# Two 256-column halves for every 512-column three-pass matmul in a hybrid decoder layer

## The chip, the cores and the metric

The kernel runs on one core of a Trainium2 chip. Its engines work side by side: TensorE multiplies matrices into PSUM, whose eight banks each hold 512 float32 columns on 128 partitions; VectorE and ScalarE read PSUM and SBUF and write the results back; GpSimd and SyncE issue most of the DMA transfers. The metric is the device time of one execution in microseconds, taken as the median of the runs.

## The reference, cut to what matters

One decoder layer for 512 tokens of width 2048, all in float32. Two attention branches (a sparse one that keeps 128 keys per query, and a dense one with a latent projection) are gated, summed and projected, and a convolutional feed-forward part of width 5632 follows:

```python
proj = h @ w_in                                   # 2048 x 7568
o_a = dsa_attention(qa, ka, va, qi, ki, wi * IDX_W_SCALE)
o_b = causal_dense_attention(mq, mk, mv)
merged = sigmoid(gate_a) * (o_a @ w_pa) + sigmoid(gate_b) * (o_b @ w_pb)
x = x + gt_a * (merged @ w_o)
u = h @ w_up                                      # 2048 x 11264
x = x + gt_f * ((silu(gate) * val) @ w_down)      # gate, val: causal convolution of u
```

Each `@` is a product that needs more precision than one fast pass of TensorE gives.

## The kernel before, in words

**Three passes.** The kernel's fast matmul format is `float32r`, a float32 of reduced precision. Every operand of the large products is split into a high part (a ScalarE copy that rounds to `float32r`) and a low part (a VectorE subtraction, the rest): `wtile` does it for weights at lines 110 and 111, `split` for activations at lines 117 and 118. `mm3` (lines 120 to 123) then adds three products into one PSUM region: high by high (line 121), high by low (line 122), low by high (line 123). Its arguments are the PSUM region `o`, the stationary pair `lh, ll` (at most 128 columns), the moving pair `rh, rl` (as many columns as `o`), and two flags: `first` starts a new sum, `last` ends it. Each matmul is one weight load of the stationary operand and one stream of the moving operand.

**Who calls it.** `lin_fm` makes blocks of 128 output features by all 512 tokens: the weights are stationary and the activations move, 512 columns. It does the branch gates, the two branch projections and `w_up`. `lin_tm` makes blocks of 128 tokens by up to 512 output features: the activations are stationary and the weights move. It does `w_o`, `w_down`, the query projection and the latents with 512 columns, and two narrower ones, 320 columns of `w_in` and 384 of `w_mq_up`. Both walk over the contraction in steps of one weight tile of up to 1104 columns, and over four banks within each step. `quarter_k` does the first part of `w_in` in the order of a written plan, while the modulation columns are still being computed. The indexer calls `mm3` with 64 rows and 256, 384 or 512 columns.

**Staging.** A weight tile is loaded by SyncE into one of five raw buffers, then split into one of three pairs of high and low buffers. The four banks `bank[0:4]` and the four `bank[4:8]` alternate between output blocks; in the attention parts the second four serve attention. When a block's contraction is done, ScalarE or VectorE empties its bank (`conv` at line 1085 for `w_up`, line 1118 for `w_down`).

**Order.** The program is written in one order, and the framework plans the order on each engine from a modelled timeline when the kernel is built; weight tiles get a priority that lets them go far ahead. In the attention parts (about 230 to 1050 us) matmuls of `mm3`, transposes and plain float32 matmuls of attention (lines 669, 677, 693, 932 to 935) alternate on TensorE. From 1050 us on the stream is almost all `mm3`; lines 752 and 753 are two single-operand matmuls that serve the modulation columns, and line 1041 transposes before the second norm. These call TensorE directly and not through `mm3`.

Of the kernel before, what the change touches and what calls it, by code (L numbers as in the profile page):

```python
# [31 lines left out]
def trunk_layer_kernel(  # L32
# [22 lines left out]
    V, A, G, PE, SP = nc.vector, nc.scalar, nc.gpsimd, nc.tensor, nc.sync  # L55
# [3 lines left out]
    psum = ctx.enter_context(tc.tile_pool(name="psum", bufs=1, space=bass.MemoryType.PSUM))  # L59
    dram = ctx.enter_context(tc.tile_pool(name="scratch", bufs=1, space=bass.MemoryType.DRAM))  # L60

# [1 line left out]
    cur = [None] * n_slots  # L63
    free = deque(range(n_slots))
    held = {}
# [1 line left out]
    def get(dt=F32):  # L67
        i = free.popleft()
        if cur[i] is None or cur[i].dtype != dt:
            cur[i] = pool.tile([P, T], dt, name=f"slot{i}", tag=f"slot{i}")  # L70
        held[id(cur[i])] = i
        return cur[i]

    def getr():
        return get(F32R)
# [42 lines left out]
        V.tensor_tensor(dst_lo, src, r32(dst_hi), ALU.subtract)  # L118

    def mm3(o, lh, ll, rh, rl, first, last):  # L120
        PE.matmul(o, lh, rh, start=first, stop=False)  # L121
        PE.matmul(o, lh, rl, start=False, stop=False)  # L122
        PE.matmul(o, ll, rh, start=False, stop=last)  # L123

    def lin_fm(src, c0, act, K, banks, evac, tick=None, M=4):
        kn = 8 // M
        for kg in range(0, K, kn):
            wh, wl = wtile(src, kg, kn, c0, M * P)
            for m in range(M):
                ms = slice(m * P, (m + 1) * P)  # L130
                for i in range(kn):
                    k = kg + i
                    ah, al = act[k]
                    mm3(banks[m], wh[:, i, ms], wl[:, i, ms], ah, al, k == 0, k == K - 1)
                if kg + kn == K:
                    evac(m, banks[m])
            if tick:
                tick()

    def lin_tm(src, c0, n, act, K, banks, evac, k0=0, tick=None):  # L140
        for kg in range(0, K, 2):
            wh, wl = wtile(src, k0 + kg, 2, c0, n)
            for tb in range(4):
                ts = slice(tb * P, (tb + 1) * P)
                for i in range(2):
                    k = kg + i
                    ah, al = act[k]
                    mm3(banks[tb][:, :n], ah[:, ts], al[:, ts], wh[:, i, :], wl[:, i, :],
                        k == 0, k == K - 1)
                if kg + 2 == K:  # L150
                    evac(tb, banks[tb][:, :n])
            if tick:
                tick()
# [2 lines left out]
        cnt["half"] += 1  # L156
        return bank[4:8] if cnt["half"] % 2 == 0 else bank[0:4]

# [1 line left out]
    ident = pool.tile([P, P], F32, name="ident")  # L160
    make_identity(nc, ident)
    ones = pool.tile([P, 1], F32, name="ones")
# [45 lines left out]
    c_act = pool.tile([P, KD], F32, name="c_act")  # L208
    PE.transpose(bank[7][:, 0:16], v1[0:16, P:2 * P], ident[0:16, 0:16])
    A.activation(c_act, bank[7][:, 0:16], AF.Silu)  # L210
    # causal bias: zeros, then the triangle of the diagonal block
    zslot = get()
    Z = zslot[:, 0:256].bitcast(BF)
    G.memset(Z, 0.0)
# [5 lines left out]
        V.tensor_scalar(v, ss, 1.0 / n, EPS, op0=ALU.mult, op1=ALU.add)  # L220
        G.tensor_tensor(dst, v, mhalf[:, :w], ALU.pow)

# [1 line left out]
    ssx = pool.tile([P, 16], F32, name="ssx")  # L224
    rstd = pool.tile([P, 4], F32, name="rstd")
    junk = get()
# [37 lines left out]
    for r in xs:  # L264
        put(*r)

# [1 line left out]
    mod = pool.tile([P, 96], F32, name="mod")  # L268
    s_a = pool.tile([P, KD], F32, name="s_a")
    s_f = pool.tile([P, KD], F32, name="s_f")  # L270
# [39 lines left out]
        V.scalar_tensor_tensor(s_a[:, 2 * g:2 * g + 2], mod[:, 16 + 2 * g:18 + 2 * g], 1.0,  # L310
                               col1[:, 96 + 2 * g:98 + 2 * g], op0=ALU.add, op1=ALU.mult)

    # input projection in quarters of the contraction: A = indexer, B = sparse k/v and part of the gates
    part = {"A": [get() for _ in range(7)], "B": [get() for _ in range(7)]}

    def quarter_k(j, w):
# [19 lines left out]
        if name == "A":  # L336
            for tb in range(1, 4):
                ts = slice(tb * P, (tb + 1) * P)
                for cb in range(2):
                    ns = slice(cb * 512, (cb + 1) * 512)  # L340
                    i = (tb - 1) * 2 + cb
                    mm3(bank[i], hh[:, ts], hl[:, ts], wh[:, ns], wl[:, ns], first, last)
                    fin(i, bank[i])
            mm3(bank[6][0:80, :], wh[:, 1024:1104], wl[:, 1024:1104], hh, hl, first, last)
            fin(6, bank[6][0:80, :], 80)
        else:
            for tb in range(4):
                ts = slice(tb * P, (tb + 1) * P)
                mm3(bank[tb], hh[:, ts], hl[:, ts], wh[:, 0:512], wl[:, 0:512], first, last)
                fin(tb, bank[tb])  # L350
            for m in range(3):
                ms = slice(512 + m * P, 512 + (m + 1) * P)
                mm3(bank[4 + m], wh[:, ms], wl[:, ms], hh, hl, first, last)
                fin(4 + m, bank[4 + m])
# [59 lines left out]
    V.tensor_copy(wcv, bank[7][:, 0:352].rearrange("p (j n) -> p j n", j=4))  # L414
    put(v2)

# [1 line left out]
    pos_f = gslot[0:4, 384:384 + P]  # L418
    V.tensor_copy(pos_f, posi)
    PE.transpose(bank[7][:, 256:260], pos_f, ident[0:4, 0:4])  # L420
# [73 lines left out]
        cnt["at"] += 1  # L494
        return AT[cnt["at"] % 4]

# [1 line left out]
    kit = part["A"][6]  # L498
    kw_tm = tslot[3][:, 0:320].rearrange("p (t n) -> p t n", t=4)
    kdup = tslot[4].rearrange("p (t a d) -> p t a d", t=4, a=2)  # L500
# [20 lines left out]
    for tb in range(1, 4):  # L521
        S = (tb + 1) * P
        qiT = []
        for cb in range(2):
# [5 lines left out]
            o = (getr(), getr())  # L530
# [4 lines left out]
        rl = [get(), get(), get()]  # L535
# [38 lines left out]
    put(*kiT, tslot[3], tslot[4])  # L574
    mask[0] = Z[:, 384:512]

# [1 line left out]
    sq = [get(), get()]  # L578

    def head_ss(dst, src3, i):  # L580
# [47 lines left out]
    for cb in range(2):  # L628
        lin_tm(w_in, C_QA + cb * 512, 512, h, KD, MM, ev_qa(cb))

# [1 line left out]
    att = {}  # L632

    def attend_bufs():
# [67 lines left out]
    put(mslot, tslot[0])  # L702
    attend_free()

# [1 line left out]
    ada_blocks = [8, 9, 10, 11, 16, 17, 18, 19, 12, 13, 14, 15, 20, 21, 22, 23]  # L706
    gst = [get(), get()]
    ada_acc = [get(), get()]
# [1 line left out]
    def ada_stream():  # L710
        for n, cb in enumerate(ada_blocks):
            assert len(pend) < 2
            acc = ada_acc[n % 2]
            for kp in range(8):
                t = raw_tile()[:, 0:1024].rearrange("p (k n) -> p k n", k=2)
                SP.dma_start(t, w_ada[kp * 2 * P:(kp + 1) * 2 * P, cb * 512:(cb + 1) * 512]
                             .rearrange("(k p) n -> p k n", p=P))
                for i in range(2):
                    k = kp * 2 + i
                    if k == 0:  # L720
                        V.tensor_scalar(acc, t[:, i], c_act[:, 0:1], None, op0=ALU.mult)
                    else:
                        V.scalar_tensor_tensor(acc, t[:, i], c_act[:, k:k + 1], acc,  # L723
                                               op0=ALU.mult, op1=ALU.add)
                yield None
            pend.append((cb, acc))
            done[0] += 1
            if done[0] == 12:
                yield None
# [3 lines left out]
    stream = ada_stream()  # L733
# [33 lines left out]
    def reload(d):  # L767
        pairs = []
        for dh, dl in d:
            th, tl = getr(), getr()  # L770
            G.dma_start(th, dh)
            G.dma_start(tl, dl)
            pairs.append((th, tl))
        return pairs

# [1 line left out]
    gate_d = [dram.tile([P, T], F32, name=f"gate{k}") for k in range(2 * KD)]  # L777
    for m in range(3):
        G.dma_start(gate_d[m], part["B"][4 + m])
# [17 lines left out]
    for n in range(GA1):  # L797
        gate_block(n)

# [1 line left out]
    krot = pool.tile([P, 4, 64], F32, name="krot")  # L801
    ss_kr = pool.tile([P, 4], F32, name="ss_kr")
    kvT = [(getr(), getr()) for _ in range(2)]
# [38 lines left out]
    lat_T(ml2, mqT, gmq)  # L842
    put(*ml2)

# [1 line left out]
    pairs = {}  # L846

    def up_pair(hp):
# [92 lines left out]
        put(*qT)  # L941
        put(*kTr, *qTr)

    # first branch projection, kept in DRAM
    pa_d = [dram.tile([P, T], F32, name=f"pa{k}") for k in range(KD)]

    def pa_block(cb):
# [24 lines left out]
    put(*gst)  # L972
    put(tslot[1], tslot[2], zslot)

# [1 line left out]
    ob = reload(ob_d) + [tuple(att["o"][0:2]), tuple(att["o"][2:4])]  # L976
    mg = []

# [30 lines left out]
    for t in ob:  # L1009
        put(*t)  # L1010

# [1 line left out]
    ss1 = pool.tile([P, 16], F32, name="ss1x")  # L1013
    x1_d = [[dram.tile([P, T], F32, name=f"x1_{db}_{tb}") for tb in range(4)] for db in range(4)]
    x1 = []
# [62 lines left out]
        put(t)  # L1078
    put(rbc2)

# [1 line left out]

    def conv(j, b):
        t = get()
# [105 lines left out]
```

## Time and profile before

| what | value |
|---|---|
| median of 2 runs | 2796.87 us (2795.78 to 2797.96) |
| span of the profiled execution | 2791.8 us |
| TensorE matmuls | 12,160, busy 2753.4 us (99%) |
| TensorE weight loads | 12,160, busy 2204.5 us (79%) |
| VectorE, ScalarE, GpSimd | busy 56%, 32%, 6% |
| memory read and written | 376.93 MB and 30.41 MB, 146 GB/s |

The profile is one execution. A line of a group names the source line, the engine, the operation, output and inputs by the program's names, the shapes, the count, then busy time and mean duration of one, and the idle time before. Matmuls are pipelined: a matmul's record reaches from its start to its modelled end, and the next one starts earlier than that. So durations overlap, and the rate is read from the distances between starts. PEld is TensorE's weight load, which has its own rows. "Issue" is a wait for nothing that the profile shows.

The profiled execution's own time isn't listed apart from its span; the median lies 5.1 us above the span, for what comes ahead of the first and behind the last recorded instruction.

### The profile page before, as it was taken

The page shows a single profiled execution, that of the slowest core. Times are in us where ns is not written, and L with a number is a line of the kernel's source. Part 1 is how long each engine was busy: PE and PEld are TensorE (multiplying, and loading weights), DVE is VectorE, ACT ScalarE, POOL GpSimd, SP SyncE. Part 2 cuts the span into 40 slices and gives each one's busy share as a digit, 9 for nine tenths or more (in the row PEclk, how much of TensorE's full clock was granted, in tenths as well). Part 3 has the DMA queues.
Part 4 walks back from the last instruction along what each step waited for, and adds up shares of the span by engine and source line. Part 5 has one row for each costly group of instructions (what it writes and reads, how often), then busy time and mean ns, then how long its engine had stood idle before and what let it go on. Part 6 is the DMA issues. An engine that isn't in the chain of part 4 may idle for free.

```text
span 2791.8 us, 31818 instructions
## 1 busy us (share of the span) xinstructions
PE 2753.4 (99%) x12160; PEld 2204.5 (79%) x12160; DVE 1550.7 (56%) x2615; ACT 903.2 (32%) x1309; POOL 177.5 (6%) x355
## 2 busy tenths in 40 slices
PE   6999999999999999999999999999999999999999
PEld 5877777788887768887888888888888888888887
DVE  7987975544467658546444353635263544434357
ACT  4333433322344553224333222222223231313231
POOL 1000100100031231000000000000000000000010
PEclk8999999999999999999999999999999999999999
DMA  9942245655464587645333433334343333333352
GB/s 321 362 138 87 68 138 176 203 188 174 151 204 132 161 293 255 207 153 186 91 98 103 123 106 113 121 106 122 98 129 98 114 98 99 97 92 98 97 168 98
DMA packets 222604, 409.43 MB, mean 147 GB/s; under 512 B 16714, under 2 KB 58084, under 8 KB 222452
## 3 DMA queue, kind: packets, MB, share of 16 engines
q1 hardware_dynamic: 200628, 348.59, 40.0%
q0 software_dynamic: 21792, 58.81, 6.2%
q8 instruction: 95, 1.56, 0.2%
q14 instruction: 57, 0.47, 0.1%
q10 hardware_dynamic: 32, 0.01, 0.0%
HBM read 376.93 MB, written 30.41 MB: 146 GB/s over the span
## 4 chain that ended last, share of the span: by engine, by line
PE 53%; DVE 0%; ACT 0%; issue 0%
PE bank L121 18%; PE bank L123 17%; PE bank L122 17%; DVE slot L1114 0%; DVE slot L1113 0%; PE bank L240 0%; ACT slot L1043 0%; PE bank L752 0%; PE bank L753 0%; ACT slot L1075 0%; PE bank L1041 0%
## 5 line engine op out<-in xcount | busy, mean ns | idle before, releaser
L111 DVE TENSOR_TENSOR wlo<-raw,whi 128x1024 fp32r<-128x1024 f32 (+2 forms) x462 | 558.2, 1209 | 868.6 <-ACT whi L110 865.6
L110 ACT ACTIVATE whi<-raw 128x1024 fp32r<-128x1024 f32 (+2 forms) x462 | 483.8, 1049 | 1418.4 <-PE bank L122 755.7
L121 PE MATMUL bank<-slot,whi 128*128 128x512 f32 (+1 forms) x2192 | 868.4, 398 | 2.7 <-ACT slot L1075 1.5
L122 PE MATMUL bank<-slot,whi 128*128 128x512 f32 (+1 forms) x2192 | 866.3, 395 | 0.0
L123 PE MATMUL bank<-slot,wlo 128*128 128x512 f32 (+1 forms) x2192 | 861.7, 396 | 0.0
L121 PE MATMUL bank<-whi,slot 128*128 128x512 f32 (+2 forms) x1472 | 572.1, 392 | 7.2 <-ACT slot L384 6.5
L122 PE MATMUL bank<-wlo,slot 128*128 128x512 f32 (+2 forms) x1472 | 575.6, 391 | 0.0
L123 PE MATMUL bank<-whi,slot 128*128 128x512 f32 (+2 forms) x1472 | 566.1, 389 | 0.0
L123 PEld LDWEIGHTS bank<-slot,wlo 128*128 128x128 f32 (+1 forms) x2192 | 411.0, 188 | 99.4 <-issue 1.9
L121 PEld LDWEIGHTS bank<-slot,whi 128*128 128x128 f32 (+1 forms) x2192 | 410.7, 187 | 98.7 <-ACT whi L110 2.1
L122 PEld LDWEIGHTS bank<-slot,whi 128*128 128x128 f32 (+1 forms) x2192 | 411.1, 188 | 96.8 <-issue 1.3
L121 PEld LDWEIGHTS bank<-whi,slot 128*128 128x128 f32 x1472 | 278.1, 189 | 71.4 <-ACT slot L384 6.7
L122 PEld LDWEIGHTS bank<-wlo,slot 128*128 128x128 f32 x1472 | 278.2, 189 | 59.2 <-issue 0.2
L123 PEld LDWEIGHTS bank<-whi,slot 128*128 128x128 f32 x1472 | 276.9, 188 | 60.7 <-issue 0.9
L723 DVE SCALAR_TENSOR_TENSOR slot<-raw,c_act,slot 128x512 f32<-128x512 f32 x240 | 179.9, 749 | 175.8 <-DMA raw<-in_w_ada 172.8
L1118 DVE TENSOR_TENSOR slot<-slot,bank 128x512 f32<-128x512 f32 x144 | 95.3, 681 | 22.8 <-PE bank L123 22.6
L298 DVE SCALAR_TENSOR_TENSOR slot<-slot,c_act,slot 128x512 f32<-128x512 f32 x110 | 78.7, 746 | 5.7 <-DMA slot<-in_w_ada 5.0
L1085 ACT ACTIVATE slot<-bank,wcv 128x512 f32<-128x512 f32 x88 | 68.0, 773 | 32.6 <-PE bank L123 32.6
L117 ACT ACTIVATE slot<-slot 128x512 fp32r<-128x512 f32 x76 | 47.3, 624 | 78.3 <-DVE slot L998 28.0
L1086 DVE SCALAR_TENSOR_TENSOR slot<-bank,wcv,slot 128x511 f32<-128x511 f32 x88 | 65.5, 744 | 3.8 <-ACT slot L1085 1.3
L1087 DVE SCALAR_TENSOR_TENSOR slot<-bank,wcv,slot 128x510 f32<-128x510 f32 x88 | 65.6, 746 | 1.9
L756 POOL DMA_DIRECT2D slot<-in_b_ada x8 | 4.4, 551 | 911.5 <-ACT whi L110 865.9
(252 smaller groups left out, 1594.8 us busy)
## 6 DMA issues: line engine op xcount, KB each, us to landing
raw<-in_w_up SPq DMA_DIRECT2D x176, 512.0 KB, 3.7
raw<-in_w_ada SPq DMA_DIRECT2D x128, 512.0 KB, 3.9
raw<-in_w_down SPq DMA_DIRECT2D x88, 512.0 KB, 3.6
raw<-in_w_in SPq DMA_DIRECT2D x82, 512.0 KB, 3.7
slot<-in_w_ada SPq DMA_DIRECT2D x128, 256.0 KB, 6.0
raw<-in_w_o SPq DMA_DIRECT2D x32, 512.0 KB, 4.7
raw<-in_w_in SPq DMA_DIRECT2D x16, 552.0 KB, 6.9
gate<-slot POOLq DMA_DIRECT2D x32, 256.0 KB, 3.8
```

Source lines behind the costliest of these rows:

```text
L110: A.activation(hi, raw[:, :w], AF.Copy)
L111: V.tensor_tensor(lo, raw[:, :w], r32(hi), ALU.subtract)
L117: A.activation(dst_hi, src, AF.Copy)
L121: PE.matmul(o, lh, rh, start=first, stop=False)
L122: PE.matmul(o, lh, rl, start=False, stop=False)
L123: PE.matmul(o, ll, rh, start=False, stop=last)
L298: stt[g] = V.scalar_tensor_tensor(acc, raw, c_act[:, k:k + 1], acc, op0=ALU.mult, op1=ALU.add)
L723: V.scalar_tensor_tensor(acc, t[:, i], c_act[:, k:k + 1], acc, op0=ALU.mult, op1=ALU.add)
L1085: A.activation(t, b, AF.Identity, bias=wcv[:, 3, j:j + 1], scale=wcv[:, 2, j:j + 1])
L1086: V.scalar_tensor_tensor(t[:, 1:], b[:, :T - 1], wcv[:, 1, j:j + 1], t[:, 1:], op0=ALU.mult, op1=ALU.add)
L1087: V.scalar_tensor_tensor(t[:, 2:], b[:, :T - 2], wcv[:, 0, j:j + 1], t[:, 2:], op0=ALU.mult, op1=ALU.add)
L1118: V.tensor_tensor(t, t, b, ALU.add)
```

## The change

`mm3` looks at the width of its output. Below 512 columns it does what it did. At 512 columns it goes over the two halves of the bank: first all three passes for columns 0 to 255, then all three for columns 256 to 511. Only the very first matmul of the first half carries the start flag; the second half's first matmul writes to a bank that the first half has already started. The framework's check on groups of matmuls is switched off for these. Sums, operands and the operations that read the banks are the same; some comments elsewhere in the file are blanked, so line numbers behind `mm3` move by four.

```diff
     def mm3(o, lh, ll, rh, rl, first, last):
-        PE.matmul(o, lh, rh, start=first, stop=False)
-        PE.matmul(o, lh, rl, start=False, stop=False)
-        PE.matmul(o, ll, rh, start=False, stop=last)
+        n = o.shape[1]
+        cut = [slice(0, n)] if n < 512 else [slice(0, 256), slice(256, 512)]
+        skip = n == 512
+        for i, c in enumerate(cut):
+            PE.matmul(o[:, c], lh, rh[:, c], start=first and i == 0, stop=False, skip_group_check=skip)
+            PE.matmul(o[:, c], lh, rl[:, c], start=False, stop=False, skip_group_check=skip)
+            PE.matmul(o[:, c], ll, rh[:, c], start=False, stop=last, skip_group_check=skip)
```

## The prediction

> **What bounds the kernel now.** I read the page first: the busy times, the row of the granted clock, and the chain that ended last.
>
> ```profile
> span 2791.8 us, 31818 instructions
> PE 2753.4 (99%) x12160; PEld 2204.5 (79%) x12160; DVE 1550.7 (56%) x2615; ACT 903.2 (32%) x1309; POOL 177.5 (6%) x355
> ...
> PEclk8999999999999999999999999999999999999999
> ...
> PE 53%; DVE 0%; ACT 0%; issue 0%
> PE bank L121 18%; PE bank L123 17%; PE bank L122 17%; DVE slot L1114 0%; DVE slot L1113 0%; PE bank L240 0%; ACT slot L1043 0%; PE bank L752 0%; PE bank L753 0%; ACT slot L1075 0%; PE bank L1041 0%
> ```
>
> TensorE is busy for 99% of the span at a clock that is full from the second slice on, and the chain holds the three passes of `mm3` (lines 121 to 123) and hardly anything else. But busy says little here, since matmuls overlap. How long one really costs is read from the distance between starts. I take the windows view of a stretch of the feed-forward part, and a few lines of the timeline from the same part.
>
> ```profile
> 2060.00:2290.00 230.00, 230.00 (x993) 186.06 (x992) 95.54 (x110) 59.69 (x66) 0.54 (x1) 1.00 0.37 113
> ```
>
> ```profile
> 2000.16 0.39 PE L122 MATMUL bank<-slot,whi 128*128 128x512 f32 x1
> 2000.16 0.19 PEld L123 LDWEIGHTS bank<-slot,wlo 128*128 128x128 f32 x1
> 2000.39 0.39 PE L123 MATMUL bank<-slot,wlo 128*128 128x512 f32 x1
> 2000.39 0.19 PEld L121 LDWEIGHTS bank<-slot,whi 128*128 128x128 f32 x1
> ```
>
> In the windows row the columns are stretch, its length, then busy time and count of TensorE, its weight loads, VectorE, ScalarE and GpSimd. In 230 us 992 weight loads were made, one for each matmul: **231.9 ns** from one 512-column matmul to the next, though a record shows 390. The timeline shows how the load fits: the load for pass 123 starts when pass 122 starts, takes 190 ns in the record, and is over before the next start 230 ns later. VectorE is busy for 96 of the 230 us and ScalarE for 60; nothing but TensorE's own rate sets the pace. So the question is only what two halves of 256 columns cost, each with its own load.
>
> **The change, part by part.** First, how many matmuls are cut. The groups by line and shape give the first pass; the other two have the same counts.
>
> ```profile
> L121 PE MATMUL bank<-slot,whi 128*128 128x512 f32 x2176 | 862.1, 398 | 2.7 <-ACT slot L1075 1.5 <-ACT whi L110 1.3
> ...
> L121 PE MATMUL bank<-whi,slot 128*128 128x512 f32 x1344 | 530.9, 398 | 6.9 <-ACT slot L384 6.5 <-ACT whi L110 0.4
> ...
> L121 PE MATMUL bank<-slot,slot 64*128 64x512 f32 x16 | 7.2, 503 | 1.8 <-ACT slot L543 1.8
> ...
> L121 PE MATMUL bank<-slot,whi 128*80 128x512 f32 x16 | 6.3, 395 | 0.0
> ```
>
> Three passes of 2176 + 1344 + 16 are **10,608** matmuls (the 48 of the indexer, with 64 rows, add a fraction of a microsecond and are left out). They become 21,216 of half the width. Every matmul has its load even where two neighbours share the stationary operand (12,160 of each on the page), so 10,608 loads are added too.
>
> No row shows a 256-column matmul of this kind with 128 rows. The nearest rows are narrower ones of the same three passes. The projection of 320 columns runs in one piece from the first row below to the 512-column matmul in the second, three passes of 64:
>
> ```profile
> 661.89 0.31 PE L121 MATMUL bank<-whi,slot 128*128 128x320 f32 x1
> ...
> 690.08 0.40 PE L121 MATMUL bank<-whi,slot 128*128 128x512 f32 x1
> ...
> L121 PE MATMUL bank<-whi,slot 128*128 128x320 f32 x64 | 19.6, 309 | 0.0
> ```
>
> That is 28.19 us for 192, 146.8 ns each. Between 320 and 512 columns a column thus costs (231.9 - 146.8) / 192 = 0.443 ns, and 64 columns fewer than 320 give 146.8 - 28.4 = **118.4 ns**. Two halves take 236.9, which is 5.0 ns over the 231.9 of the whole: the fixed part of a matmul, paid once more. This assumes that the line goes on to 256 columns, where the weight load could become the limit. The indexer has 256-column passes with 64 rows:
>
> ```profile
> 234.75 0.19 PEld L121 LDWEIGHTS bank<-slot,slot 64*128 64x128 f32 x1
> 234.86 0.28 PE L121 MATMUL bank<-slot,slot 64*128 64x256 f32 x1
> 234.87 0.18 PEld L122 LDWEIGHTS bank<-slot,slot 64*128 64x128 f32 x1
> 234.98 0.28 PE L122 MATMUL bank<-slot,slot 64*128 64x256 f32 x1
> 234.98 0.19 PEld L123 LDWEIGHTS bank<-slot,slot 64*128 64x128 f32 x1
> 235.10 0.28 PE L123 MATMUL bank<-slot,slot 64*128 64x256 f32 x1
> ```
>
> Three passes into the same 256 columns of one bank start 120 ns apart, each with its load in between; adding to columns that were written 120 ns earlier costs nothing visible. So a half lies between 116 (half of 231.9, no fixed part) and 120: **0 to +86 us**. I take 118.4, which comes from 128 rows and the same operands and lies between: 10,608 x 5.0 = **+53 us**.
>
> How fast can loads follow one another? Transposes, whose 128 columns stream in less time, show it:
>
> ```profile
> 1302.04 3.65 PE L1041 MATMUL bank<-ident,slot 128*128 128x128 f32 x32
> ```
>
> With 0.27 us for the last one's own record, 31 steps take 3.38 us: 109 ns for a load and its matmul. A half of 118.4 ns hides such a load with 9 ns to spare, where a whole matmul had 123. If that cover is gone, a nanosecond over 118.4 costs 21 us.
>
> Two rules of the Trainium skill bear on this. Its page "TensorE: Matmul & The Clock Gate", in the section on packing small matmuls, says that a weight load overlaps matmuls in flight only when the row group differs. By its figures (columns over 1.2 GHz for a load, over 2.4 GHz for the stream) a half would then cost an estimated 107 + 107 ns and the change over a millisecond. The trace disagrees, since the loads above run under matmuls of the same 128 rows, and 230 ns would not hold both parts. The same page, under "Back-to-back issue gap", gives columns over 2.4 GHz plus 2.5 ns; by that estimate the fixed part is 2.5 ns and the change costs 27 us. The rows here put it at 5.0.
>
> Next, fetching instructions. TensorE's own go from 24,320 to 45,632 (the indexer's 48 counted).
>
> ```profile
> q8 instruction: 95, 1.56, 0.2%
> ```
>
> This queue moves 1.56 MB now, 64 bytes for each of the 24,320; it will move 2.9 MB, at 0.4% of the DMA engines. I cost it at nothing: 95 packets over the span are one in 29 us, so the stretch of 230 us above holds some eight of them, and it averages the same 231.9 ns as the steps of the timeline between them. After the change a packet comes every 15 us. The bank is written and read whole as before, so the operations that empty it wait for the last half and start when they did, within a few ns; VectorE and ScalarE have over half their time free to hide it. The first matmuls run at half the clock:
>
> ```profile
> 44.08 0.63 PE L121 MATMUL bank<-whi,slot 128*128 128x512 f32 x1
> 44.51 0.63 PE L122 MATMUL bank<-wlo,slot 128*128 128x512 f32 x1
> ```
>
> That is 430 ns each, where the fixed part disappears; some twenty matmuls, nothing.
>
> What can move is the order. TensorE's order is planned when the kernel is built, from modelled costs, and in the attention parts it mixes `mm3` with narrow matmuls. A switch of row count shows an uncovered load:
>
> ```profile
> 846.68 0.38 PE L935 MATMUL bank<-slot,slot 64*128 64x256 f32 x1
> ...
> 846.90 0.28 PE L932 MATMUL bank<-slot,slot 64*128 64x256 f32 x1
> ...
> 847.02 0.28 PE L933 MATMUL bank<-slot,slot 64*128 64x256 f32 x1
> ...
> PEld bank L935 <- issue: 12.1, 23, 0.8
> ...
> PEld bank L121 <- issue: 9.3, 30, 0.4
> ```
>
> The step after the switch is 0.22 us instead of 0.12. The two largest groups of such gaps hold 53 of them and 21.4 us. If the new plan makes half as many more, or fewer, that is **±11 us**; I take zero and keep it for the range.
>
> The sum: 2791.8 + 53 = 2845 of span. The median of the runs is 2796.9, 5.1 us more than the profiled span, which is what lies around it; so **2850 us, +1.9%**. Two per cent, 56 us, is about what a measurement of this kernel can tell from no change, and the forecast lies just inside it.
>
> **The rivals.**
>
> *Issue becomes the limit* (slower). TensorE has to take in a load and a matmul every 118 ns, without pause, for over two milliseconds. For it: the longest proof of such a rate is the 32 transposes above, which may have been queued while earlier, wider matmuls ran; the longest sustained stretch, the 192 of 320 columns, shows only 146.8 ns a pair. Against it: nothing slows within those 32. It decides from 118.4 ns a pair on. The rows bound it by 118.4 and 146.8; the middle, 132.6, gives 2 x 132.6 - 231.9 = 33.3 ns on each of 10,608, **+353 us, 3150**. The Trainium skill's TensorE page, under "Wait — 56ns, not 53.3ns?", gives 62 ns per matmul for its sequencer's software decoding; if a load took as much, a pair would be an estimated 124 ns and the time 2968, and no run here shows that.
>
> *Loads in series* (slower by far). If a load kept the weight path for its whole recorded 188 ns, two halves would take 376: +1529 us, 4326. The 320-column stretch, at 146.8 ns with the same loads, is against it.
>
> *No fixed part.* At 116 ns a half the time stays 2797. The 320-column rows are against it: 5/8 of 231.9 is 144.9, not 146.8.
>
> *Faster.* If narrow matmuls streamed at the 109 ns of the transposes, two would take 218: -147 us, 2650. The 120 ns of the 64-row passes speak against it.
>
> **How the numbers follow.** The forecast has 0.80, issue 0.09, serial loads 0.02, no fixed part 0.05, faster 0.04. The forecast's own spread is 116 to 120 ns a half and the plan's ±11 us; its middle is 2850, and 2853 is the 2% line, so I put 0.34 of its 0.80 above. Slower: 0.34 + 0.09 + 0.02 = 0.45. Same: 0.46 + 0.05 = 0.51. Faster: 0.04. The range runs up to 2890 (120 ns gives 2883, and part of the plan's 11) and down to 2820: 117 ns, +22 us, is 2819, about as far below 118.4 as the 64-row rows lie above. Outside it stay the rivals and little else.
>
> **What would show it.** After the change, a pure stretch of the feed-forward part should have a load and a matmul each 118 to 119 ns, with records near 0.28 us for a matmul; TensorE's counts should be 22,816. If starts lie at 124 or more, with loads that begin late, issue is the limit; if at 109, the fixed part was a cost of width. If the pure stretches fit and the total doesn't, the attention parts between 230 and 1050 us were reordered. The forecast is wrong if 256 columns don't lie on the line through 320 and 512.

## The result

The changed kernel took 2863.7 us in its first two runs (2859.9 and 2867.4) against 2796.9, a ratio of **1.0241** [1.0224, 1.0257]. Measured once more beside the kernel before (2794.6), four runs gave 2854.3, a ratio of **1.0221** [1.0205, 1.0236]. The change costs about 60 to 67 us and lies just beyond 2%; its runs scatter more, from 2853.7 to 2867.4, than those of the kernel before, from 2791.1 to 2798.7. The intervals are some 0.15% to either side, so a change far below 2% can be told from none here.

The page of the changed kernel, its first profile:

```profile
span 2865.6 us, 53164 instructions
...
PE 2811.9 (98%) x22816; PEld 2743.8 (96%) x22816; DVE 1550.6 (54%) x2615; ACT 906.7 (32%) x1311; POOL 178.5 (6%) x355
...
PEclk8999999999999999999999999999999999999999
...
q8 instruction: 178, 2.92, 0.4%
...
PE 52%; DVE 0%; ACT 0%; issue 0%
```

TensorE has the 22,816 matmuls and loads that were counted, and the instruction queue has its 2.9 MB. VectorE and ScalarE do what they did. The weight loads are now busy for 96% instead of 79%, and yet the chain is still TensorE's, with nothing put down to issue. TensorE idles for 2865.6 - 2811.9 = 53.7 us, where it was 38.4 before.

The same stretch of the feed-forward part in the windows view (stretch, length, then busy time and count of TensorE, its loads, VectorE, ScalarE, GpSimd), and the timeline of the changed kernel:

```profile
2060.00:2290.00 230.00, 230.00 (x1949) 229.91 (x1948) 106.15 (x129) 59.75 (x66) 1.08 (x2) 1.00 0.37 112
```

```profile
2000.20 0.28 PE L126 MATMUL bank<-slot,whi 128*128 128x256 f32 x1
2000.20 0.19 PEld L127 LDWEIGHTS bank<-slot,wlo 128*128 128x128 f32 x1
2000.31 0.28 PE L127 MATMUL bank<-slot,wlo 128*128 128x256 f32 x1
2000.32 0.19 PEld L125 LDWEIGHTS bank<-slot,whi 128*128 128x128 f32 x1
2000.43 0.28 PE L125 MATMUL bank<-slot,whi 128*128 128x256 f32 x1
```

1948 loads in 230 us are **118.1 ns** a half, where the line through wider matmuls had given 118.4. Each load starts with the matmul before it. Its record of 0.19 us reaches past the start of its own matmul 0.11 us later, so the record is longer than the time for which a load holds that matmul up, and 96% busy doesn't mean that the loads are the limit. Over all undisturbed steps of the second half of the span the mean is 118.0 ns for a half and 232.1 ns for a whole: cutting costs 2 x 118.0 - 232.1 = **3.9 ns**, and 10,608 times that is 41 us. The other 18 to 26 us had to be found.

Where the time goes is seen at the transposes ahead of the second norm (minimum, median and longest in ns, then first and last start in us), in the kernel before and in the changed kernel's second profile, whose span is 2852.0 us:

```profile
L1041 PE MATMUL bank<-ident,slot x64: 271/273/331, 1302.0 to 1312.6; 128*128 128x128 f32 x64
```

```profile
L1045 PE MATMUL bank<-ident,slot x64: 270/273/328, 1337.3 to 1347.3; 128*128 128x128 f32 x64
```

Behind the last of them lie 1479.2 us before (2791.8 - 1312.6) and 1504.7 after (2852.0 - 1347.3): +25.5, and the 6336 cut matmuls there explain 6336 x 3.9 = 24.7. Ahead of it the change costs 34.7 us, though only 4272 matmuls are cut there, which explains 17. So the fixed part explains the feed-forward part fully, and half of the rest. (These are single profiles. In the four runs below that change the feed-forward part alone, the last of these transposes started at 1311.9 to 1315.6 us, so some 3 us ahead of it are a matter of the execution.)

### The profile page after: what moved, and what is told of

The parts are those of the page before. It is cut to its first block, busy times and chain, and to the rows that moved or that the text cites. A ratio compares the mean times of both kernels' runs of the same rounds, so it can differ in the third digit from the quotient of the medians.

```text
span 2865.6 us, 53164 instructions
## 1 busy us (share of the span) xinstructions
PE 2811.9 (98%) x22816; PEld 2743.8 (96%) x22816; DVE 1550.6 (54%) x2615; ACT 906.7 (32%) x1311; POOL 178.5 (6%) x355
## 4 chain that ended last, share of the span: by engine, by line
PE 52%; DVE 0%; ACT 0%; issue 0%
PE bank L126 17%; PE bank L127 17%; PE bank L125 17%; DVE slot L1117 0%; DVE slot L1118 0%; PE bank L244 0%; ACT slot L1047 0%; PE bank L756 0%; PE bank L757 0%; DVE slot L1080 0%; ACT slot L1079 0%; PE bank L1045 0%
## 5 line engine op out<-in xcount | busy, mean ns | idle before, releaser
L126 PE MATMUL bank<-slot,whi 128*128 128x256 f32 (+1 forms) x4384 | 1238.4, 283 | 0.0
L125 PE MATMUL bank<-slot,whi 128*128 128x256 f32 (+1 forms) x4384 | 1232.7, 282 | 2.5 <-ACT slot L1079 1.5
L127 PE MATMUL bank<-slot,wlo 128*128 128x256 f32 (+1 forms) x4384 | 1233.2, 282 | 0.3 <-DVE wlo L111 0.3
L125 PEld LDWEIGHTS bank<-slot,whi 128*128 128x128 f32 (+1 forms) x4384 | 827.0, 189 | 6.6 <-issue 2.1
L126 PEld LDWEIGHTS bank<-slot,whi 128*128 128x128 f32 (+1 forms) x4384 | 824.9, 188 | 3.8 <-issue 2.3
L127 PEld LDWEIGHTS bank<-slot,wlo 128*128 128x128 f32 (+1 forms) x4384 | 823.4, 188 | 4.6 <-issue 2.1
L125 PE MATMUL bank<-whi,slot 128*128 128x256 f32 (+2 forms) x2816 | 797.5, 284 | 16.1 <-ACT slot L388 6.4
L126 PE MATMUL bank<-wlo,slot 128*128 128x256 f32 (+2 forms) x2816 | 800.5, 285 | 0.0
L127 PE MATMUL bank<-whi,slot 128*128 128x256 f32 (+2 forms) x2816 | 795.5, 284 | 0.0
L125 PEld LDWEIGHTS bank<-whi,slot 128*128 128x128 f32 x2816 | 532.4, 189 | 18.7 <-ACT slot L388 6.5
L126 PEld LDWEIGHTS bank<-wlo,slot 128*128 128x128 f32 x2816 | 533.3, 189 | 2.3 <-issue 1.3
L127 PEld LDWEIGHTS bank<-whi,slot 128*128 128x128 f32 x2816 | 530.1, 189 | 2.1 <-issue 1.0
L1089 ACT ACTIVATE slot<-bank,wcv 128x512 f32<-128x512 f32 x88 | 68.0, 772 | 31.3 <-PE bank L127 31.3
```

What stands on the lines that cost most here:

```text
L125: PE.matmul(o[:, c], lh, rh[:, c], start=first and i == 0, stop=False, skip_group_check=skip)
L126: PE.matmul(o[:, c], lh, rl[:, c], start=False, stop=False, skip_group_check=skip)
L127: PE.matmul(o[:, c], ll, rh[:, c], start=False, stop=last, skip_group_check=skip)
L1089: A.activation(t, b, AF.Identity, bias=wcv[:, 3, j:j + 1], scale=wcv[:, 2, j:j + 1])
```

## The experiments

The theory: a fixed part for every added matmul, and a second part, ahead of the feed-forward part only, that comes from another order of TensorE's instructions. In the two programs TensorE's order differs: the last logits of the sparse attention stand behind 1816 matmuls of `mm3` before, and behind 1585 (counted in whole widths) after, by the starts in the traces. The main rival: everything goes with the number of cuts.

**Cut only one part of the kernel.** A switch is set for each run, off at the start and on from the feed-forward part for the first, the reverse for the second:

```diff
-        cut = [slice(0, n)] if n < 512 else [slice(0, 256), slice(256, 512)]
-        skip = n == 512
+        skip = n == 512 and hv["on"]
+        cut = [slice(0, 256), slice(256, 512)] if skip else [slice(0, n)]
...
+    hv["on"] = True
     acc_f = [[None] * 4 for _ in range(4)]
```

> Halves only in the convolutional feed-forward part (w_up and w_down, 6336 of the 10,608 full-row 512-column matmuls); ahead of it TensorE's planned order is that of the kernel before. Theory (a fixed part of 4.0 ns for each added matmul, and a changed order of TensorE's work ahead of the feed-forward part worth some 24 us): 6336 x 4.0 = +25 us, 2822 us, a ratio of 1.009. Rival (the whole +66.8 us goes with the number of matmuls that are cut): 66.8 x 6336 / 10,608 = +40 us, 2837 us, 1.014.

> Halves only ahead of the feed-forward part (4272 matmuls); TensorE's planned order there is that of the changed kernel. Theory (fixed part plus order): 4272 x 4.0 = 17 us and some 24 us of order, +41 us, 2838 us, 1.015. Rival (all in proportion to the number of matmuls cut): +27 us, 2824 us, 1.010.

The feed-forward part alone: 2821.3 us, 1.0087 [1.0074, 1.0101], +24.9 us, 3.9 ns for each of its 6336, as the theory said, and away from the rival's 1.014. The rest alone: 2828.2 us, 1.0116 [1.0102, 1.0129], +31.8 us. By its number alone the second run is nearer to the rival's 2824 than to the theory's 2838. What the rival cannot give is both runs together: with two thirds as many cuts the second costs more, where 3.9 ns for each of its 4272 would be 17 us. The theory's order part had been sized from the first two runs of the changed kernel, which are its slowest.

**Exchange the orders.** With edges between TensorE's instructions, each program is made to issue in the other's order: the halves where their passes stood before, and the whole matmuls where their first halves stand after.

```diff
+    trace = [i for i in nc.cur_bb.bb.instructions if i.engine == PE.engine and type(i).__name__ == "InstMatmult"]
...
+        if prev is not None:
+            tc.add_manual_dep(trace[at], prev.name,
+                              mybir.DependencyInfo(mybir.DependencyClass.NoSync, mybir.DependencyReason.DATA),
+                              reason="order")
+        prev = trace[at]
```

> All halves of the change, but TensorE is made to issue in the order of the kernel before: each half stands where its pass stood. Theory (order is the second part): only the fixed part is left, 10,608 x 4.0 = +42 us, 2839 us, 1.015. Rival (the order costs nothing, the rest is load traffic or clock): as the changed kernel, +67 us, 2864 us, 1.024.

> No halves at all, 512-column matmuls as in the kernel before, but TensorE is made to issue in the order of the changed kernel. Theory (order is the second part): +24 us, 2821 us, 1.009. Rival (the order costs nothing): no change, 2797 us, 1.000.

> The changed kernel once more, to narrow its interval and see how far its executions scatter. Both theories: 2860 to 2867 us, 1.022 to 1.026.

Halves in the old order: 2843.7 us, 1.0168 [1.0154, 1.0182], +47.3 us. Whole matmuls in the new order: 2806.1 us, 1.0038 [1.0025, 1.005], **+9.6 us** without a single cut. The order has a cost of its own, and taking it back returns part of the loss. Both are off the theory's sizes: the order alone costs 10 us and not 24, and the halves without it 47 and not 42. Together, 47.3 + 9.6 = 56.9, they make up the 59.7 us that the changed kernel cost when it was measured once more, since each of the three is uncertain by some 4 us. Those 2854.3 us are themselves below the 2860 to 2867 that were expected. Between the first profile of the changed kernel and the second lie 13.6 us, and 12.2 of them ahead of the last transpose (1359.5 and 1347.3 us).

What the new order costs is seen in the waits of TensorE and of its loads (total us, times, longest) in the run with whole matmuls and the new order, and in the line of the timeline for the longest:

```profile
PE bank L151 <- ACT slot L640: 6.4, 1, 6.4
...
PEld bank L151 <- issue: 12.6, 43, 0.4
```

```profile
313.26 0.79 PE L151 MATMUL bank<-whi,slot 128*128 128x512 f32 x1 [6.40 <-ACT slot L640]
```

Line 640 there is line 610 of the kernel before, the copy of a query projection's bank: TensorE now reaches the next projection before that bank has been emptied, and waits 6.4 us for it. ScalarE is late with the copy because it waits for VectorE, which is at work on the choice of the keys (lines 597 and 598):

```profile
311.10 0.69 ACT L635 ACTIVATE slot<-bank,col 128x512 f32<-128x512 f32 x1 [2.25 <-DVE slot L597]
...
312.61 0.60 ACT L640 ACTIVATE slot<-bank 128x512 f32<-128x512 f32 x1 [0.82 <-DVE slot L598]
```

The kernel before has no such wait of a matmul, and 0.4 us of a load. In the changed kernel (second profile) it is there, at line 614, and so is one for the copy of a gate's bank (line 786 of the kernel before):

```profile
PE bank L125 <- ACT slot L614: 5.5, 1, 5.5
...
PE bank L756 <- DVE slot L790: 2.6, 1, 2.6
```

The row `PEld bank L151 <- issue` above counts loads that stood uncovered at the first pass of `mm3`: 43 times for 12.6 us, where the kernel before had 30 for 9.3. I sorted all steps between starts of full-row `mm3` matmuls ahead of the feed-forward part: the time at the clean rate of their width (3.9 ns and 0.4457 ns a column, from the steps of 118.0 and 232.1), what steps took beyond it where that is at most 0.3 us (an uncovered load, or a step at half the clock) and where it is more (a wait), and the steps that begin with another matmul. All in us, worked out from the starts in each trace. The 320- and 384-column steps have the same clean rate in all, which is left out.

| kernel | last transpose | clean rate | up to 0.3 us beyond (steps) | of that at half the clock | waits | other matmuls |
|---|---|---|---|---|---|---|
| before | 1312.6 | 991.5 | 25.8 (234) | 4.1 (22) | 8.7 | 222.9 |
| halves in the feed-forward part alone | 1315.4 | 991.5 | 27.3 (241) | 5.2 (28) | 7.1 | 224.8 |
| whole, new order | 1325.2 | 991.5 | 31.3 (286) | 5.0 (27) | 9.0 | 230.0 |
| halves, old order | 1338.2 | 1008.2 | 29.7 (285) | 6.7 (64) | 8.4 | 226.3 |
| changed, second profile | 1347.3 | 1008.2 | 32.6 (328) | 5.8 (57) | 14.9 | 226.4 |

The column on the clock is there because, besides the start of each kernel, it isn't full all the way. In the kernel before, matmuls of 512 columns start 0.43 us apart just before 301 us, and 0.23 apart behind:

```profile
300.01 0.63 PE L121 MATMUL bank<-whi,slot 128*128 128x512 f32 x1
300.43 0.63 PE L122 MATMUL bank<-wlo,slot 128*128 128x512 f32 x1
...
301.45 0.40 PE L122 MATMUL bank<-wlo,slot 128*128 128x512 f32 x1
301.68 0.40 PE L123 MATMUL bank<-whi,slot 128*128 128x512 f32 x1
```

The windows view has a granted clock of 0.50 there from 294.3 to 301.1 us, and each of the other profiles has such a stretch of 6.8 to 10.2 us between 298 and 321 us. A whole matmul is then 0.2 us late and a half 0.1, so the same stretch holds twice as many steps once they are cut. At the full clock there are 212, 213, 259, 221 and 271 steps with an uncovered load.

The fixed part is +16.7 in both kernels with halves. The new order adds 4.6 us of uncovered loads at the full clock (47 steps) and 7.1 in the last column, which holds the wait of 6.4. In the changed kernel the two parts meet: 59 more uncovered steps at the full clock (+5.1), 1.7 more at half the clock, 6.2 more of waits, 3.5 in the last column.

The halves in the old order keep some 9 us over the kernel before that are neither. Few of them are uncovered loads: at the full clock those are 9 more steps (+1.3). 2.6 us are steps at half the clock, half of it because this execution had one more stretch of it, from 1042.6 to 1046.0 us; 3.4 are other matmuls, and most of the rest is spread over steps near the clean rate. One profile of each kernel stands behind the table, and executions differ: in the second row, where nothing ahead of the feed-forward part is changed, the last transpose is 2.8 us later than before, and against that row 6 us are left. What makes them stays open. Only TensorE's order was given back, too: of VectorE's 2615 instructions, 2222 are, by their names, the same operation as the one in their place in the kernel before (1532 in the changed kernel). Whether that plays a part was not tried.

**Change the size of the pieces.** In the feed-forward part alone the cut is moved, to find where the weight load shows. The first run cuts at column 272, the second in the same way at 384.

```diff
-        cut = [slice(0, n)] if n < 512 else [slice(0, 256), slice(256, 512)]
-        skip = n == 512
+        skip = n == 512 and hv["on"]
+        cut = [slice(0, 272), slice(272, 512)] if skip else [slice(0, n)]
```

> As the run with halves in the feed-forward part alone, but the cut is at column 272: pieces of 272 and 240 columns. Theory (a matmul costs 0.443 ns a column and a fixed part; the load is hidden): the sum is the same, 2822 us, 1.009. Rival (118 ns at 256 columns is the time of a weight load, which nothing narrower can go below): 125.4 + 118 = 243.4 ns for a pair, 11.3 ns over the whole, 6336 x 11.3 = +72 us, 2869 us, 1.026.

> As before with pieces of 384 and 128 columns. The line through 320 and 512 columns gives 175.2 + 61.7 = 236.9 ns, 2825 us, 1.010, if no load showed. Theory (loads are hidden only down to the 109 ns of the transposes): 175.2 + 109 = 284.2 ns, 52 over the whole, 6336 x 52 = +330 us, 3127 us, 1.118. Rival (a load takes 118): 293.2 ns, +387 us, 3184 us, 1.138.

At 272 and 240 columns: 2831.7 us, 1.0132 [1.0117, 1.0147], +37.1 us. At 384 and 128: 3141.7 us, 1.1245 [1.1229, 1.1262], +347.1 us. The first is 12 us over the two equal halves, which the theory had not expected, and 37 under the rival, so 118 ns was not the time of a load; the mean steps in its trace are 125.5 to 126.0 ns for 272 columns and 111.6 to 112.2 for 240. The second is near the theory's 3127. Its timeline shows why it is a little over:

```profile
2000.65 0.19 PEld L127 LDWEIGHTS bank<-slot,whi 128*128 128x128 f32 x1
2000.82 0.22 PE L127 MATMUL bank<-slot,whi 128*128 128x128 f32 x1
2000.82 0.19 PEld L128 LDWEIGHTS bank<-slot,whi 128*128 128x128 f32 x1
2000.88 0.28 PE L128 MATMUL bank<-slot,whi 128*128 128x128 f32 x1
2000.93 0.19 PEld L129 LDWEIGHTS bank<-slot,wlo 128*128 128x128 f32 x1
2000.99 0.27 PE L129 MATMUL bank<-slot,wlo 128*128 128x128 f32 x1
2001.04 0.19 PEld L127 LDWEIGHTS bank<-slot,whi 128*128 128x128 f32 x1
2001.10 0.39 PE L127 MATMUL bank<-slot,whi 128*128 128x384 f32 x1
```

The matmul at 2000.82 is followed by the next after 0.06 us, so 128 columns do stream in that time. From then on the loads set the pace, one each 0.11 us (2000.82, .93, 2001.04), and the matmuls follow them. So a load takes 109 to 112 ns here, 240 columns stand just at that, and 256 columns have 6 to 9 ns to spare. The Trainium skill, on its page "TensorE: Matmul & The Clock Gate" under "LDWEIGHTS (loading the stationary operand)", gives columns over 1.2 GHz, an estimated 107 ns for 128; the trace agrees within 2 to 5 ns.

**Change the order within a cut.** In the feed-forward part alone both halves of a pass stand side by side, so that the same columns are added to every 236 ns and not every 118.

```diff
+        for p, (a, b) in enumerate(((lh, rh), (lh, rl), (ll, rh))):
+            for i, c in enumerate(cut):
+                PE.matmul(o[:, c], a, b[:, c], start=first and i == 0 and p == 0, stop=last and p == 2,
+                          skip_group_check=skip)
```

> Halves in the feed-forward part alone, but both halves of a pass stand side by side (first pass on the left half, first pass on the right half, second pass on the left ...), so that the same columns are added to every 236 ns and not every 118. Theory (the fixed part belongs to each matmul): 2822 us as with halves one after the other, 1.009. Rival (adding to columns written 118 ns before costs the 4 ns): no extra cost, 2797 us, 1.000.

2819.6 us, 1.0095 [1.0078, 1.0111], as with the halves one after the other (1.0087 [1.0074, 1.0101]); the mean step is 118.2 ns. The fixed part doesn't come from adding to fresh sums. It belongs to the matmul with its load; which of the two carries it could not be told apart, since each matmul of this format brings its own load.

## Why the prediction was right

- **What bounds.** Right. TensorE's rate sets the pace before and after; VectorE's and ScalarE's work moved by nothing that shows, and the prefetch of instructions, twice as dense (178 packets, one in 16 us), left no gap in the 230 us stretch. One reading was too coarse: a 9 in the row of the clock stands for 90% or more of a slice, and the clock was not full from the second slice on, but at half from 294.3 to 301.1 us. The sum isn't moved by it, since every profile has such a stretch.
- **The price of a half.** Right in mechanism, a little over in size: the line gave 118.4 ns and 5.0 ns for the cut, the trace has 118.0 and 3.9. The term of +53 us measured 41; in the feed-forward part, where it stands alone, 24.9 us.
- **The cover of the weight load.** Right: 109 ns of load under 118 of matmul. Pieces of 240 columns stand at the edge and 128 are bound by the load.
- **The order, taken at zero with ±11 us.** This is the term that was mis-sized. By itself the new order cost 9.6 us, and with the halves in place the uncovered loads, waits and other matmuls ahead of the feed-forward part came to 16.5 us over those of the kernel before. The mechanism that the prediction named, more places where a load isn't covered, is there (212 to 271 steps at the full clock), but waits of TensorE for banks that are still full joined it, and those it had not named. Some 6 us of the halves in the old order are neither, and stay open.
- **The sum.** 53 + 0 against some 41 + 19: the two errors partly cancel, which is luck, and 2850 stood 4 to 14 us under the medians, which lie inside the range. The 5.1 us that it added to the span are not what lies around it: where a run's time and span are both on record, they differ by 1.8 us (2867.4 and 2865.6), so the profiled execution was itself some 3 us faster than the median. To forecast the median, adding them was right even so. The side of the 2% line, which the prediction put at nearly even chances, came out slower.
- **The rivals.** Issue as the limit is refuted: 118.0 ns a pair held for 1500 us. Serial loads and no fixed part are refuted by the same row, and so is 109 ns a half. The two rules of the page "TensorE: Matmul & The Clock Gate" of the Trainium skill fared as follows. Against the one under "Packing small matmuls", loads do run under matmuls of the same rows. By the one under "Back-to-back issue gap", a start would come an estimated 215.8 ns after another at 512 columns and 109.2 at 256; the traces have 232.1 and 118.0, and the fixed part in them is 3.9 ns, between that rule's 2.5 and the 5.0 of the line.

## What to carry to other kernels

A matmul's price is the distance between starts, and two or three widths in one trace give a line from which another width can be read, as long as it stays above the time of its weight load (109 to 112 ns here); halving the widest matmul pays the small fixed part once more and hides nothing new. Where the framework plans the order of instructions, a change of their number or size can also be a change of order, here in the mixed stretches ahead of the feed-forward part: budget for it (it cost 9.6 us by itself here), and separate it by running each set of instructions in the other's order.

## What the runs showed that was not expected

In the first profile of the changed kernel the clock fell to half shortly after the second norm. The windows view of that place with TensorE alone (busy time and count, granted clock, DMA share, GB/s), and the timeline:

```profile
1361.60:1366.20 4.60, 4.55 (x27) 0.65 0.00 0
```

```profile
1361.22 0.74 PE L125 MATMUL bank<-slot,whi 128*128 128x256 f32 x4 [1.45 <-ACT slot L1079]
...
1363.37 0.42 PE L126 MATMUL bank<-slot,whi 128*128 128x256 f32 x1
1363.58 0.41 PE L127 MATMUL bank<-slot,wlo 128*128 128x256 f32 x1
...
1366.48 0.28 PE L126 MATMUL bank<-slot,whi 128*128 128x256 f32 x1
1366.60 0.28 PE L127 MATMUL bank<-slot,wlo 128*128 128x256 f32 x1
```

Halves are 0.21 us apart and then 0.12 again; 16 of them cost 1.5 us. Two halves at half the clock take 0.43 us, as a whole matmul does in the prediction's row of 44 us: there the cut costs nothing, as the prediction had said. What precedes is ten microseconds of transposes and an idle step of 1.45 us. The kernel before has the same stretch, and its clock stayed full:

```profile
1312.50:1317.00 4.50, 3.05 (x16) 1.00 0.21 79
```

The same profile has another such dip from 1083.1 to 1086.5 us, with no transposes in the ten microseconds ahead of it, but an idle step of 2.45 us. In the second profile TensorE idles 2.59 us at the same place, and the clock stays full.

```profile
1082.29 0.50 PE L756 MATMUL bank<-slot,ones_r 128*128 128x512 f32 x1 [2.45 <-DVE slot L790]
...
1083.77 0.41 PE L125 MATMUL bank<-slot,whi 128*128 128x256 f32 x1
1083.98 0.41 PE L126 MATMUL bank<-slot,whi 128*128 128x256 f32 x1
```

So whether such a dip comes is a matter of the execution. The Trainium skill, on its page "TensorE: Matmul & The Clock Gate" under "PE-mode transpose", says that transposes don't count as busy for the clock gate in the same way. The first dip would fit that, but the second came without transposes, so the runs here don't show it.
